# Strassen blocks added to x as woven work, and the second layer's query latent in one pass over k-tiles 8 to 15, then 0 to 7

## The chip, the core and the metric

One NeuronCore of one Trainium2 chip runs the whole program as one launch. The metric is device microseconds (us) of one execution. PE is TensorE, PEld its weight loads, DVE is VectorE, ACT ScalarE, POOL GpSimd, SP SyncE, whose queue issues nearly all loads. PSUM is used as eight banks of 128 x 512 floats.

## What is computed

A trunk of two layers over 256 tokens (x is 256 x 2048, float32), all weights float32. Each layer, cut to what matters here:

```
h    = rmsnorm(x);  proj = h @ w_in        # 2048 -> 4928: c_q (512), c_kv (256), k_rope (64), rq, rk, rv, rg
mix  = concat(rmsnorm(latent attention(c_q, c_kv, k_rope)), retention(rq, rk, rv, rg))
x    = x + mix @ w_o
h    = rmsnorm(x)
x    = x + square(relu(h @ w_up)) @ w_down # 2048 -> 8192 -> 2048
```

After the second layer there is a last rmsnorm. `c_q` is the query latent.

## The kernel before

x stays on the chip, transposed, as 16 tiles `x[0]` to `x[15]` of 128 features x 256 tokens. Every weight passes once through the same line (`stream`, L216): SP loads 512 KB into one of five `raw` buffers, ACT rounds it to a high half (L195), DVE subtracts to get the low half (L196), both into one of six `w` buffers, and PE multiplies. I call that a chunk and its two halves its split. `mac_feat` (L227) is one pair of matmuls: L229 takes the weight's high half against both halves of the activation (512 columns), L230 the low half against one (256 columns). An activation tile `xs[j]` is made from `x[j]` by `norm_tile` (L333: ACT L191, DVE L192). The sum of squares that the norm needs is gathered by `add_square` (L267: ACT L272, DVE L273 into `ssq`); the norm itself is applied later, as row factors (`scale_rows`, L399; its first matmuls are L306).

The MLP runs in four blocks of 2048 hidden features. In each, `w_up` gives 16 tiles `us`; then `w_down` is done in two ways. Output tiles 0 to 7 come from a Strassen step: eight times (k = 0 to 7) 21 matmuls of 512 columns (`seven_products`, L722, matmul L730) into seven banks, from sums and differences of the weights that DVE makes in place in `raw` (L716). Output tiles 8 to 15 are plain, each 16 pairs over two chunks (`next_tile`, L808), placed between the Strassen steps. In the last block of a layer the seven sums are joined on DVE (`join_products`, L740, L747) into four 128 x 512 blocks of tokens, and `add_blocks` (L750) adds those to `x[0]` to `x[7]`: for each tile two transposes on PE (L756) into a bank and one DVE addition (L757), then `done_x` (L674), which makes `xs` and the square for the next layer. In that last block the sums of blocks 0 to 2 are joined and added once more, before the second `w_up` group (L787).

At the end of a layer six plain tiles stand behind steps k = 0 to 5 (`LAST_TILE_AFTER`); after step 7 come tile 14, `add_blocks`, tile 15. In the second layer the latent `cq` then takes two passes (L368 and L369) of two output tiles each over all k-tiles, in chunks of four k-tiles from the back (12 to 15 first). Then follow the 320 columns of c_kv and k_rope (L380 to L385), which I call the kv stage, and rq, rk, rv, rg.

Tasks that need little PE are written as generators and put in `woven`; `stream` calls `weave` (L201) after each chunk's matmuls, and each call runs one generator to its next `yield`.

The order on each engine is not that of the source alone. A list scheduler of the framework orders instructions by its own costs when the program is built, and each engine then runs its queue strictly in that order, waiting on semaphores. So the order is read from the built program.

## Time and profile before

| | |
|---|---|
| median of 3 runs | 2172.16 us (2171.90 to 2172.17) |
| the profiled execution, its own time | 2172.12 us |
| its span | 2170.3 us (1.8 us lie around it) |
| PE, DVE, ACT busy | 98%, 82%, 60% of the span |
| largest stretch with PE waiting | 1059 to 1094 us, the change of layers |

The profile's page gives the averages; a window view gives busy time and the granted PE clock of a stretch; the timeline gives each instruction's start and duration, with the idle time ahead of it and what ended it in brackets. Successive instructions of one engine overlap in the records: the step from start to start is what one costs in a row, and the duration is a little more.

### The profile page before, as it was taken

How to read it: one execution, taken by the hardware profiler on the slowest of the kernel's cores; microseconds unless marked ns; L12 is line 12 of the kernel's file. 1: busy time of each engine (PE TensorE's matmuls, PEld its weight loads, DVE VectorE, ACT ScalarE, POOL GpSimd, SP SyncE). 2: the span in 40 equal slices, each digit the busy share in tenths (PEclk: the TensorE clock that was granted, in tenths of full speed). 3: DMA queues.
4: the chain of work that ended last, by engine and by line, in shares of the span. 5: the costliest groups of instructions: out<-in, count | busy, mean ns of one | idle time of the engine just before them, and what ended most of it. 6: DMA issues, size and time to landing. Idle time of an engine off the chain costs nothing.

```text
span 2170.3 us, 32892 instructions
## 1 busy us (share of the span) xinstructions
PE 2135.7 (98%) x11926; PEld 1861.6 (86%) x11926; DVE 1789.4 (82%) x3183; ACT 1300.3 (60%) x2234; POOL 107.0 (5%) x130
## 2 busy tenths in 40 slices
PE   7999999999999999999899999999999999999997
PEld 6888888888888888888688888888888888888886
DVE  8878976788689779879968888676986887898797
ACT  7455545565676566566645555456665655665665
POOL 4000000001001001100000000000010010010000
PEclk9999999999999999999999999999999999999998
DMA  7555456658757857855465555566587577577663
GB/s 247 171 161 174 147 189 196 184 168 227 235 165 216 241 165 217 247 176 173 148 200 159 165 173 165 183 189 186 169 236 219 167 224 236 165 217 224 181 194 107
DMA packets 364771, 412.69 MB, mean 190 GB/s; under 512 B 14144, under 2 KB 284608, under 8 KB 364608
## 3 DMA queue, kind: packets, MB, share of 16 engines
q1 hardware_dynamic: 349824, 397.08, 59.7%
q0 software_dynamic: 13824, 12.59, 3.9%
q8 instruction: 93, 1.52, 0.3%
q10 hardware_dynamic: 960, 0.92, 0.1%
q14 instruction: 70, 0.57, 0.1%
HBM read 395.85 MB, written 2.10 MB: 183 GB/s over the span
## 4 chain that ended last, share of the span: by engine, by line
PE 88%; DVE 7%; ACT 2%; issue 1%; DMA 1%; SPq 0%; DVEq 0%; ACTq 0%
PE mm L229 43%; PE mm L230 22%; PE mm L730 11%; PE mm L234 3%; DVE w L196 2%; DVE raw L716 2%; PE mm L235 1%; PE at L229 1%; ACT w L195 1%; DMA raw<-w_down 1%; PE at L230 1%; PE at L500 0%; PE at L499 0%; PE mm L383 0%; PE mm L384 0%
## 5 line engine op out<-in xcount | busy, mean ns | idle before, releaser
L195 ACT CAST w<-raw 128x1024 fp32r<-128x1024 f32 (+2 forms) x856 | 847.1, 1007 | 656.8 <-PE mm L230 363.2
L196 DVE TENSOR_TENSOR w<-raw,w 128x1024 fp32r<-128x1024 f32 (+2 forms) x856 | 987.1, 1170 | 291.9 <-ACT w L195 286.1
L229 PE MATMUL mm<-xs,w 128*128 128x512 f32 x2944 | 1034.2, 394 | 8.5 <-ACT w L195 8.3
L230 PE MATMUL mm<-xs,w 128*128 128x256 f32 x2944 | 827.4, 281 | 4.4 <-DVE w L196 4.4
L229 PEld LDWEIGHTS mm<-xs,w 128*128 128x128 f32 x2944 | 553.8, 188 | 127.8 <-ACT w L195 8.6
L230 PEld LDWEIGHTS mm<-xs,w 128*128 128x128 f32 x2944 | 556.0, 189 | 7.5 <-DVE w L196 7.1
L229 PE MATMUL mm<-u,w 128*128 128x512 f32 x1024 | 360.7, 393 | 0.2 <-ACT w L195 0.2
L230 PE MATMUL mm<-u,w 128*128 128x256 f32 x1024 | 288.8, 282 | 6.4 <-DVE w L196 6.4
L229 PEld LDWEIGHTS mm<-u,w 128*128 128x128 f32 x1024 | 193.2, 189 | 43.0 <-ACT w L195 0.7
L230 PEld LDWEIGHTS mm<-u,w 128*128 128x128 f32 x1024 | 194.0, 189 | 10.0 <-DVE w L196 7.3
L730 PE MATMUL mm<-w,f 128*128 128x512 f32 x768 | 191.1, 396 | 2.2 <-ACT w L195 1.2
L716 DVE TENSOR_TENSOR raw<-raw 128x512 f32<-128x512 f32 x256 | 176.8, 691 | 6.6
L229 PE MATMUL mm<-mix,w 128*128 128x512 f32 x512 | 178.0, 391 | 0.0
L730 PEld LDWEIGHTS mm<-w,f 128*128 128x128 f32 x768 | 144.0, 188 | 38.9 <-ACT w L195 2.1
L820 POOL DMA_DIRECT2D x<-t x96 | 83.4, 869 | 1863.0 <-ACT t L819 1561.9
L230 PE MATMUL mm<-mix,w 128*128 128x256 f32 x512 | 143.7, 281 | 0.0
L247 ACT COPY tb<-mm 128x256 f32<-128x256 f32 x232 | 82.5, 371 | 63.0 <-PE mm L230 59.3
L229 PEld LDWEIGHTS mm<-mix,w 128*128 128x128 f32 x512 | 96.1, 188 | 20.8
L730 PE MATMUL mm<-w,u 128*128 128x512 f32 x384 | 110.6, 396 | 0.0
L248 DVE TENSOR_TENSOR t<-mm,tb 128x256 f32<-128x256 f32 x232 | 91.4, 418 | 19.9 <-ACT tb L247 19.4
L230 PEld LDWEIGHTS mm<-mix,w 128*128 128x128 f32 x512 | 96.4, 188 | 0.0
L234 PE MATMUL mm<-w,xs 128*128 128x512 f32 x256 | 92.8, 401 | 0.0
(202 smaller groups left out, 1955.3 us busy)
## 6 DMA issues: line engine op xcount, KB each, us to landing
raw<-w_up SPq DMA_DIRECT2D x256, 512.0 KB, 4.4
raw<-w_down SPq DMA_DIRECT2D x256, 512.0 KB, 5.2
raw<-w_in SPq DMA_DIRECT2D x144, 512.0 KB, 4.5
raw<-w_o SPq DMA_DIRECT2D x64, 512.0 KB, 4.1
x<-t POOLq DMA_DIRECT2D x96, 128.0 KB, 5.7
raw<-w_uq SPq DMA_DIRECT2D x16, 384.0 KB, 4.3
raw<-w_in SPq DMA_DIRECT2D x16, 320.0 KB, 3.2
raw<-w_ukv SPq DMA_DIRECT2D x8, 512.0 KB, 4.3
```

Of the source, the lines that this page charges most:

```text
L195: nc.scalar.copy(dst_h, src)
L196: nc.vector.tensor_tensor(dst_l, src, dst_h.bitcast(F32), op=ALU.subtract)
L229: nc.tensor.matmul(ps, wk[:, 0, n0:n0 + P], act.rearrange("p s t -> p (s t)"), start=first, stop=False)
L230: nc.tensor.matmul(ps[:, 0:T], wk[:, 1, n0:n0 + P], act[:, 0, :], start=False, stop=last)
L234: nc.tensor.matmul(ps, act[:, 0, t0:t0 + P], wk, start=first, stop=False)
L235: nc.tensor.matmul(ps[:, 0:256], act[:, 1, t0:t0 + P], wk[:, 0], start=False, stop=last)
L247: nc.scalar.copy(tb, ps[:, T:2 * T])
L248: nc.vector.tensor_tensor(dst, ps[:, 0:T], tb, op=ALU.add)
L716: nc.vector.tensor_tensor(dst, dst, other, op=ALU.add)
L730: nc.tensor.matmul(ps[i], a[:, p, :], w[:, q, :], start=first and n == 0, stop=last and n == 2)
L820: nc.gpsimd.dma_start(x[j], t, accum_op=ALU.add)
```

## The change

`add_blocks` becomes a generator that yields ahead of every second (or third) tile, so that its transposes and additions are woven between chunks. It is used so in three places: for blocks 0 to 2 inside the second `w_up` group of each layer's last block; at the end of layer 1 inside the latent of layer 2; at the end of layer 2 inside plain tiles 14 and 15 (three tiles a piece). In layer 1 seven plain tiles stand behind steps 0 to 6, and tile 15 follows step 7. The latent of layer 2 is one pass of four output tiles, in chunks of two k-tiles, over k-tiles 8 to 15, then 0 to 7, built at the end of layer 1. The squares of x for layer 2 are no longer made in `done_x`; they are woven into the kv stage, in the order 8 to 15, 0 to 7.

```diff
-TILE_AFTER, LAST_TILE_AFTER = range(8), range(6)
+TILE_AFTER, LAST_TILE_AFTER = range(8), (range(7), range(6))
-    def stream(w, r0, c0, nk, width=256, kc=None, backward=False):
+    def stream(w, r0, c0, nk, width=256, kc=None, first=0):
-        for s in reversed(range(0, nk, kc)) if backward else range(0, nk, kc):
+        for s in [*range(first, nk, kc), *range(0, first, kc)]:
...
+    def first_squares(first):
+        for i, j in enumerate([*range(first, KD), *range(first)]):
+            if i % 4 == 0:
+                yield
+            add_square(acc, x[j], i == 0)
+    latent = None
...
-            if l == 0:
-                woven["a"].append(first_squares())
+            woven["a"].append(first_squares(SN if l else 0))
...
-                for ps in proj_feat(w_in[l], 0, c0, xs, backward=l > 0):
+                for ps in proj_feat(w_in[l], 0, c0, xs) if latent is None else [latent.pop(0) for _ in range(2)]:
...
                 if not last_layer:
                     xs_n[j] = norm_tile(j, (l + 1) * G_LAYER + G_ATTN)
-                    add_square(acc_n, x[j], not squared)
...
-            def add_blocks(blocks, final=True):
+            def add_blocks(blocks, final=True, start=0, step=2):
                 for n in range(2):
                     for f in range(SB // P):
                         j = n * (SB // P) + f
+                        if j == start:
+                            start += step
+                            yield
                         xT = abank()
...
                     if end and c == 4:
-                        add_blocks(join_products(sums, sums), False)
+                        woven["a"].append(add_blocks(join_products(sums, sums), False))
...
-                    if k in (LAST_TILE_AFTER if end else TILE_AFTER):
+                    if k in (LAST_TILE_AFTER[l] if end else TILE_AFTER):
                         next_tile()
...
                 if end:
                     blocks = join_products(pp, sums)
-                    while len(tiles) > 1:
-                        next_tile()
-                    add_blocks(blocks)
+                    if last_layer:
+                        woven["a"].append(add_blocks(blocks, step=3))
                 else:
                     gather_products(pp, sums, b == 0)
                 while tiles:
                     next_tile()
+            if not last_layer:
+                woven["a"].append(add_blocks(blocks))
+                next(woven["a"][0])
+                latent = proj_feat(w_in[l + 1], 0, COL_CQ, xs_n, 4, SN)
+            finish("a")
             acc, xs = acc_n, xs_n
```

The places in the built order that the prediction speaks of follow. The numbers behind the names tell buffers apart (`x6_85` is the pair of tiles 6 and 7, `p4` a joined block, `mm` and `at` banks); `w<-raw,w` of shape 128x8x128 is the low half of a plain tile's chunk, 128x2x512 that of a chunk of the latent with the change.

DVE, before, at the change of layers: the low half of tile 15's second chunk, with the last of what stands ahead of it.

```order
L273 TENSOR_TENSOR ssq_4164<-ssq_4164,sq_10948 128x256
L192 SCALAR_TENSOR_TENSOR xs5_10955<-x4_81,gain_73,xs5_10955 128x256
L273 TENSOR_TENSOR ssq_4164<-ssq_4164,sq_10958 128x256
L757 TENSOR_TENSOR x6_85<-x6_85,at_10961 128x256
L757 TENSOR_TENSOR x6_85<-x6_85,at_10971 128x256
L196 TENSOR_TENSOR w_11005<-raw_11003,w_11005 128x8x128
L192 SCALAR_TENSOR_TENSOR xs6_10965<-x6_85,gain_73,xs6_10965 128x256
```

DVE, with the change, at the same place: from tile 15's first chunk to the latent's second.

```order
L196 TENSOR_TENSOR w_10885<-raw_10883,w_10885 128x8x128
L248 TENSOR_TENSOR t_10825<-mm_10782,tb_10826 128x256
L747 TENSOR_TENSOR p2_5855<-p1_5853,mm_10182 128x512
L817 TENSOR_TENSOR x14_101<-x14_101,t_10825 128x256
L196 TENSOR_TENSOR w_10906<-raw_10904,w_10906 128x8x128
L196 TENSOR_TENSOR w_10939<-raw_10937,w_10939 128x2x512
L192 SCALAR_TENSOR_TENSOR xs14_10830<-x14_101,gain_73,xs14_10830 128x256
L747 TENSOR_TENSOR p6_5863<-p1_5853,mm_10186 128x512
L196 TENSOR_TENSOR w_10974<-raw_10972,w_10974 128x2x512
```

Between the two chunks of tile 15 stood 24 additions, low halves of `xs` and squares; now three additions stand there.

PE, before, at the end of the program, in the middle of tile 15: `keep_warm`'s matmuls (L850), which the scheduler put there.

```order
L229 MATMUL mm<-u_20503,w 128x512
L230 MATMUL mm<-u_20503,w 128x256
L229 MATMUL mm<-u_20696,w 128x512
L850 MATMUL mm<-u_20189,u_20199 128x512 x13
L230 MATMUL mm<-u_20696,w 128x256
L229 MATMUL mm<-u_20706,w 128x512
```

PE, with the change, at the end of tile 15 (L857 is `keep_warm`, L759 the transposes).

```order
L229 MATMUL mm<-u_21043,w 128x512
L230 MATMUL mm<-u_21043,w 128x256
L759 MATMUL at<-cst,p_16662 128x128
L857 MATMUL mm<-u_20189,u_20199 128x512 x8
L306 MATMUL at<-ones,ssq 128x1
L857 MATMUL mm<-u_20189,u_20199 128x512 x6
L306 MATMUL at<-ones,sq 128x1
```

The 13 matmuls left the tile, and the last transpose of `x[7]` now follows it.

DVE, with the change, behind the kv stage of layer 2: the last square, the copies out of the kv stage's banks, and the first instruction of the row factors (L308).

```order
L273 TENSOR_TENSOR ssq_4164<-ssq_4164,sq_11334 128x256
L196 TENSOR_TENSOR w_11621<-raw_11631,w_11621 128x128
L392 COPY kv_nat_11389<-mm_11204 128x256
L395 COPY kv_nat_11389<-mm_11204 128x2x32 x2
L392 COPY kv_nat_11390<-mm_11205 128x256
L395 COPY kv_nat_11390<-mm_11205 128x2x32 x2
L308 TENSOR_SCALAR v6_11449<-at_11451 128x2
```

Fifteen additions of squares moved here from the end of layer 1; before, the copies stood ahead of the 128x128 low halves, and no square was near.

## Rows read from the trace of the kernel before

**Rows 1.** The page, busy time of each engine: us (share), instructions.

```profile
PE 2135.7 (98%) x11926; PEld 1861.6 (86%) x11926; DVE 1789.4 (82%) x3183; ACT 1300.3 (60%) x2234; POOL 107.0 (5%) x130
```

**Rows 2.** Who PE waited for, 1053 to 1113 us: us in total, times, longest.

```profile
PE mm L230 <- DVE w L196: 8.0, 2, 6.4
```

**Rows 3.** Windows: us, busy of PE, PEld, DVE, ACT, POOL; clock, DMA share, GB/s.

```profile
1053.68:1112.77 59.09, 49.17 (x252) 40.71 (x251) 45.90 (x75) 31.98 (x55) 0.00 (x0) 0.91 0.52 152
...
1083.92:1089.21 5.29, 5.29 (x18) 4.61 (x19) 4.81 (x7) 0.67 (x2) 0.00 (x0) 0.50 0.62 171
1112.77:1132.40 19.63, 19.63 (x130) 18.99 (x129) 14.03 (x25) 12.01 (x23) 0.00 (x0) 1.00 0.82 240
...
922.13:932.13 10.00, 9.87 (x63) 8.70 (x62) 9.57 (x29) 8.14 (x19) 0.00 (x0) 1.00 0.28 70
```

**Rows 4.** Timeline of PE, change of layers: start, us, instruction, count, idle before.

```profile
1053.68 0.86 PE L730 MATMUL mm<-wh,u 128*128 128x512 f32 x3
1054.38 0.86 PE L730 MATMUL mm<-w,u 128*128 128x512 f32 x3
...
1067.12 0.39 PE L229 MATMUL mm<-u,w 128*128 128x512 f32 x1
...
1072.32 1.69 PE L756 MATMUL at<-cst,p 128*128 128x128 f32 x14
...
1083.92 0.58 PE L230 MATMUL mm<-u,w 128*128 128x256 f32 x1 [6.42 <-DVE w L196]
...
1112.77 0.31 PE L383 MATMUL mm<-w,xs 128*128 128x320 f32 x1
```

**Rows 5.** Timeline of DVE, change of layers.

```profile
1050.68 2.86 DVE L716 TENSOR_TENSOR raw<-raw 128x512 f32<-128x512 f32 x4
1053.46 2.50 DVE L196 TENSOR_TENSOR w<-raw,w 128x1024 fp32r<-128x1024 f32 x2
1055.88 0.42 DVE L248 TENSOR_TENSOR t<-mm,tb 128x256 f32<-128x256 f32 x1
1056.21 0.68 DVE L196 TENSOR_TENSOR wh<-raw,wh 128x512 fp32r<-128x512 f32 x1
...
1058.28 0.48 DVE L192 SCALAR_TENSOR_TENSOR xs<-x,gain,xs 128x256 fp32r<-128x256 f32 x1
...
1068.49 3.08 DVE L747 TENSOR_TENSOR p<-p,mm 128x512 f32<-128x512 f32 x5
...
1072.63 0.75 DVE L757 TENSOR_TENSOR x<-x,at 128x256 f32<-128x256 f32 x2
...
1082.64 1.22 DVE L196 TENSOR_TENSOR w<-raw,w 128x1024 fp32r<-128x1024 f32 x1
```

**Rows 6.** Timeline of PE, a break of four transposes in the retention of layer 2.

```profile
1188.10 0.60 PE L595 MATMUL at<-cst,on 128*128 128x128 f32 x4
1188.45 0.48 PE L229 MATMUL mm<-xs,w 128*128 128x512 f32 x1
```

**Rows 7.** The page, DMA issues: count, size, median us from issue to landing.

```profile
raw<-w_in SPq DMA_DIRECT2D x144, 512.0 KB, 4.5
```

**Rows 8.** Timeline of PE, blocks 0 to 2 added in layer 1's last block.

```profile
922.13 1.91 PE L756 MATMUL at<-cst,p 128*128 128x128 f32 x16
924.17 0.50 PE L229 MATMUL mm<-xs,w 128*128 128x512 f32 x1
```

**Rows 9.** Timeline of PE, end of the program.

```profile
2144.52 1.91 PE L756 MATMUL at<-cst,p 128*128 128x128 f32 x16
...
2149.30 3.15 PE L850 MATMUL mm<-u,u 128*128 128x512 f32 x13
...
2156.83 0.38 PE L306 MATMUL at<-ones,sq 128*128 128x1 f32 x2 [1.37 <-ACT sq L683]
```

**Rows 10.** Timeline of DVE, end of the program: tile 15's second split.

```profile
2150.72 1.22 DVE L196 TENSOR_TENSOR w<-raw,w 128x1024 fp32r<-128x1024 f32 x1
```

**Rows 11.** Timeline of ACT, end of the program.

```profile
2156.36 0.42 ACT L683 ACTIVATE sq<-x 128x256 f32<-128x256 f32 x1 [0.95 <-DVE x L814]
```

More of the change, by code (lines that the diff above doesn't have):

```diff
@@ L235, in mac_tok, with proj_feat @@
         nc.tensor.matmul(ps[:, 0:256], act[:, 1, t0:t0 + P], wk[:, 0], start=False, stop=last)
-    def proj_feat(w, r0, c0, acts, nt=2, backward=False):
+    def proj_feat(w, r0, c0, acts, nt=2, first=0):
         ps = [bank() for _ in range(nt)]
         nk = len(acts)
-        for i, (k, wk) in enumerate(stream(w, r0, c0, nk, nt * P, backward=backward)):
+        for i, (k, wk) in enumerate(stream(w, r0, c0, nk, nt * P, first=first)):
             for n in range(nt):
@@ L343 @@
         xs[j] = norm_tile(j, G_ATTN)
-    def first_squares():
-        for j in range(KD):
-            if j % 4 == 0:
+    def first_squares(first):
+        for i, j in enumerate([*range(first, KD), *range(first)]):
+            if i % 4 == 0:
                 yield
-            add_square(acc, x[j], j == 0)
+            add_square(acc, x[j], i == 0)
+    latent = None
     for l in range(DEPTH):
```

## The prediction

> **What bounds the kernel now.** I read four views in this order: the page, the waits of PE, windows over the stretches with waits, and the timelines of PE, DVE and ACT there. On the page PE is busy nearly throughout [rows 1], so only two kinds of gain are left: time in which PE waits, and PE work that could go. The waits of PE over the change of layers [rows 2] name one cause above all: the low half of a weight chunk, made by DVE, 8.0 us in two waits. The timeline shows the large one [rows 4]: 6.42 us at 1083.92, in the middle of plain tile 15. What DVE did instead stands in its own timeline [rows 5]: the low half that PE wants is started only at 1082.64, behind the 24 additions, xs and squares that begin at 1072.63. The window behind the wait [rows 3] then shows a second price: the granted clock is 0.50, the lower level of 1.2 GHz, for 5.29 us after the engine stood idle 6.42 us.
>
> **The change of layers, worked out.** What PE has to do between 1053.68 (first product of step 6) and 1112.77 (first matmul of the kv stage) [rows 4]:
> - 42 products of steps 6 and 7. Three take 0.70 us from start to start, so 0.233 each: 9.8 us.
> - 96 pairs (tiles 14 and 15: 32; the latent: 64). From 1067.12 to 1072.32 there are 15: 0.347 each, 33.3 us.
> - 16 transposes. Four in a break take 0.35 us, and the first matmul behind them 0.48 instead of 0.39 us [rows 6]: 0.45 for four, 1.8 us.
> - 0.1 us for each tile's slower first pair (as in [rows 6]), 0.2.
>
> The sum is 45.1 us, and the stretch took 59.09 [rows 3]: 14.0 us are lost. Of these 8.0 are the two waits for DVE [rows 2], 2.2 the lower clock (18 matmuls in 5.29 us where nine pairs take 3.1), and the remaining 3.8 short waits in step 7, where DVE has four additions in raw and four low halves to make in 4.9 us of PE.
>
> With the change the same PE work stands there, with the same loads, only in another order: tile 14 between steps 6 and 7, the transposes in four pieces. Will PE wait again? I add up DVE's queue in its new order, each instruction at its full duration [rows 5], which is an upper bound, since in a row they overlap by about a tenth. It is free of step 6 at 1055.96 (1053.46 + 2.50). Up to tile 15's second low half come seven low halves of 1024 columns (1.25), one of 512 (0.68), four additions in raw (2.86), two joins and two additions to x (0.42 each), one xs (0.48), one joined block (0.62): 15.1 us, so 1071.0. PE wants it after 21 + 21 products, tile 14 and half of tile 15: 1053.68 + 9.8 + 5.55 + 2.8 + 0.2 = 1072.0. In time by 1 us at the worst, by 2.4 if the overlap is counted. The latent's first transposes, at 1077.6, want the last joined block: 6.7 us more of DVE, 1077.7 at the worst, 1075.8 with the overlap. The fourth chunk, at 1084.4, wants xs[15]: 5.8 us more, 1083.5 at the worst. SP's queue holds as many loads as before; tile 14's two now go ahead of step 7's, and the latent's eight are 512 KB each as they were. Each needs the buffer that DVE gave back five loads earlier: the latent's second chunk that of step 7's first load, free by 1066 at the worst, and it lands 4.5 us later [rows 7], 1070.5, where DVE comes to it at 1073 or later. Nothing is late by more than some tenths, so I take **14.0 us gained** (kv stage from 1098.8). Bounds: 14.0 above, and 8.8 below, should 3 us of waits come back with their 2.2 us of lower clock.
>
> **The squares, moved.** Fifteen additions of squares and two more latent tiles (join, xs, square) land on DVE in the kv stage. DVE is busy 14.03 of the 19.63 us up to the first row-factor matmul at 1132.40 [rows 3]. 15 times 0.34 (0.42 less the overlap) and 2 times 1.05 are 7.2, so 21.2 us, less 1.2 for the copies that now stand behind the squares: 20.0 in 19.6. ACT, at 12.0, gets the same squares and tiles at about the same price, 19.2, and has a little room. So the row factors' matmul waits some tenths, and what follows it on DVE starts later by the copies. I put **0.5 us lost** here; bounds 0 and 4 (none of the excess is hidden, and the factors' broadcast is late too).
>
> **The blocks inside w_up.** Sixteen transposes in one burst take 2.04 us to the next matmul, and that one is 0.1 slower [rows 8]; four breaks of four are 1.8 [rows 6]. This occurs once in each layer: **0.5 us gained** in all, bounds 0.6 gained and 0.6 lost (a wait of 0.1 in each of the new breaks). DVE's additions there are the same in number, and PE did not wait before.
>
> **The end.** Tile 15 held 13 matmuls of keep_warm, 3.0 us [rows 9]. They hid a wait: its second low half is started at 2150.72 [rows 10], ready at 2151.9, while PE wanted it at 2149.3. In the new order it stands behind eight instructions of at most 0.42 instead of sixteen: begun at 2144.9, behind the first transposes, they and the low half take 4.6 us at the worst, 3.8 with the overlap: ready at 2148.7 to 2149.5. PE, with 15 transposes and eight pairs ahead, is there at 2149.1, so it waits 0.4 at most. So tile 15 ends at 2144.52 + 16 x 0.347 + 1.9 for transposes = 2152.0 instead of 2154.8. Not all of it reaches the end: the last transpose of x[7] now follows the tile, and ACT squares x[7] ahead of the copy with which tile 15's join begins. From 2152.0: transpose 0.3, then addition, square, copy, join, addition at about 0.4 each, with 0.3 between them: the last square starts at 2154.6 to 2154.8, before at 2156.36 [rows 11]. **1.6 us gained**; bounds 0 (the low half is as late as before, and PE waits for it) and 2.8 (the whole tile's).
>
> **The sum.** The profiled execution's own time is 2172.12 us, the median of the runs shown 2172.16, so one stands for the other. 2172.1 - 14.0 + 0.5 - 0.5 - 1.6 = **2156.5 us**. A measurement of this kernel can tell about 0.2%, 4.3 us, from no change.
>
> **The rivals.**
> - *DVE is still late at the change of layers.* The stretch has 45.9 us of DVE work [rows 3]; less about eleven squares' additions of 0.42 some 41 remain in 45.1, so there is little room, and a buffer or a load that comes late moves the whole queue. For it: my upper bounds leave 1 us or less. Against: they are upper bounds, and six steps before it lose a square each. Waits of 3 us and 2.2 us of clock: 2161.7.
> - *The squares hold up the row factors.* ACT and DVE wait for each other by turns on two buffers of squares, so the excess of 0.4 us may be 4: 2160.0.
> - *Slower: breaks of transposes lower the clock.* The place is every break that the change makes, four in each w_up group and four in the latent. After the idle time the lower level cost 0.24 us a pair (2.2 over nine). If each of the 12 breaks costs the eight pairs up to the next one that, it is 96 x 0.24 = 23.0 us: 2179.5. It decides from 16 / 0.24 = 66 pairs on. Against: in the window of 10 us from 922.13, which begins with the burst of 16, the clock is 1.00 [rows 3].
> - *It does not do what it says:* the wait only moves (to the kv stage's first chunks, say), and the time stays at 2172.
>
> On the third of these the Trainium skill speaks (TensorE: Matmul & The Clock Gate, Part 4: PE-mode transpose): the full clock does not engage for transposes, since they do not count as busy in the same way. By that rule the breaks would be idle time and the third rival would hold, 2179.5 instead of 2156.5. The one row that bears on it disagrees: 16 in a row, longer than any new break, left the clock at 1.00.
>
> **How the numbers follow.** My forecast, 2154.3 to 2158.5, has 0.65 (its width: 0.6 either way for the w_up groups, 1 for the end, 1 for the squares). Squares late by more: 0.12, 2158.5 to 2160.5. DVE still late: 0.12, 2160 to 2165, half of it below 2162. Clock: 0.03. No change: 0.03. Better than I count: 0.05. The range 2154.3 to 2162.0 holds 0.65 + 0.12 + 0.06 = 0.83. Faster by over 0.2% are all but the clock, the unchanged case: 0.94; within 0.2%: 0.03; slower: 0.03.
>
> **What would show it.** Right: PE's waits from 1053 to 1100 us below 1 us in all, the kv stage's first matmul near 1098.8, the clock at 1.00 throughout there, keep_warm's matmuls behind tile 15, the row factors' first matmul 5.5 to 6.5 us behind the last of the kv stage. Wrong: a wait for a low half in tile 15 or the latent (first rival); idle PE ahead of L306 or of the factors' broadcast (second); a clock below 1.00 with no idle time ahead of it (third); pairs in the latent slower than 0.35 us.

## The result, and the profile after

| | before | after |
|---|---|---|
| median | 2172.16 us (2171.90 to 2172.41, 4 runs) | 2154.28 us (2153.87 to 2154.59, 4 runs) |
| the profiled execution, its own time | 2172.12 us | 2153.87 us |
| its span | 2170.3 us | 2152.1 us |

The ratio is 0.9916, 95% interval 0.9904 to 0.9928: faster by 17.9 us, where 15.6 were forecast, so the time lies 0.02 us under the range that was given (2154.3 to 2162.0), and the forecast was off by 2.2 us. The direction, the place and the largest term were right; the term of the end was too small by 1 us, and the other small terms were off to the same side.

The page of the changed kernel, busy time of each engine, answers [rows 1]:

```profile
PE 2130.2 (99%) x11926; PEld 1860.1 (86%) x11926; DVE 1786.9 (83%) x3183; ACT 1301.6 (60%) x2234; POOL 108.0 (5%) x130
```

The instructions are the same in number. PE's busy time fell by 5.5 us, its idle time by the rest of the 18.2 us between the spans (which are printed to 0.1 us, so a stretch that ends with the program is good to 0.05 us). Who PE waited for over the whole program (us in total, times, longest):

```profile
PE mm L229 <- ACT w L195: 7.6, 1, 7.6
PE mm L230 <- DVE w L196: 3.2, 2, 2.5
PE at L322 <- DVE rs_y L295: 1.6, 1, 1.6
```

The first two lie in the first 24 us of the program, the third at its end. At the change of layers, where 8.0 us stood [rows 2], nothing is left. The windows from step 6 to the kv stage, and from there to the row factors' first matmul, answer [rows 3] (columns as there):

```profile
1053.10:1097.96 44.86, 44.86 (x252) 39.02 (x251) 39.34 (x60) 25.89 (x39) 0.00 (x0) 1.00 0.67 200
1097.96:1117.72 19.76, 19.76 (x130) 18.90 (x129) 19.03 (x39) 18.20 (x41) 0.00 (x0) 1.00 0.77 235
```

PE is busy in all of the 44.86 us, at a clock of 1.00. Its timeline there answers [rows 4]:

```profile
1063.53 0.86 PE L730 MATMUL mm<-wh,u 128*128 128x512 f32 x3
...
1068.42 0.39 PE L229 MATMUL mm<-u,w 128*128 128x512 f32 x1
...
1076.75 0.60 PE L759 MATMUL at<-cst,p 128*128 128x128 f32 x4
...
1079.97 0.60 PE L759 MATMUL at<-cst,p 128*128 128x128 f32 x4
```

1063.53 is step 7, 1068.42 tile 15, and two of the four breaks of transposes in the latent (L759; L756 before) follow. From one break to the next are 3.22 us: eight pairs of 0.347 and 0.44 for the break. DVE's timeline, with [rows 5]:

```profile
1062.04 3.64 DVE L196 TENSOR_TENSOR w<-raw,w 128x1024 fp32r<-128x1024 f32 x3
...
1066.91 2.35 DVE L196 TENSOR_TENSOR w<-raw,w 128x1024 fp32r<-128x1024 f32 x2
...
1071.32 3.07 DVE L747 TENSOR_TENSOR p<-p,mm 128x512 f32<-128x512 f32 x5
...
1077.24 0.74 DVE L760 TENSOR_TENSOR x<-x,at 128x256 f32<-128x256 f32 x2
...
1096.19 0.82 DVE L196 TENSOR_TENSOR w<-raw,w 128x640 fp32r<-128x640 f32 x1 [1.95 <-ACT w L195]
```

The row at 1066.91 is tile 15's second low half and the latent's first. The former is done by some 1068.1 and PE wants it at 1071.2, eight pairs into the tile; before the change it was begun at 1082.64. By 1096 DVE is ahead of PE and waits for ACT. Before the change not all of the 10.0 us ahead of that low half was work; 1.32 us went by in waiting for a copy of ACT:

```profile
1074.70 0.42 DVE L248 TENSOR_TENSOR t<-mm,tb 128x256 f32<-128x256 f32 x1 [1.32 <-ACT tb L247]
```

The stretches, each from the starts of the same instructions in the two timelines of PE:

| stretch | before | after | difference | forecast |
|---|---|---|---|---|
| start to the second w_up group of layer 1's last block | 899.92 | 899.72 | -0.20 | |
| that group (blocks 0 to 2), to step 0 | 90.97 | 90.58 | -0.39 | -0.25 |
| step 6 to the kv stage | 59.09 | 44.86 | -14.23 | -14.0 |
| kv stage to the row factors' first matmul, and the factors | 20.45 | 20.65 | +0.20 | +0.5 |
| the w_up group of layer 2, to step 0 | 90.96 | 90.65 | -0.31 | -0.25 |
| steps 6 and 7 of layer 2 | 10.56 | 9.88 | -0.68 | |
| tile 14 of layer 2 to the end | 31.45 | 28.85 | -2.60 | -1.6 |

The other stretches agree within 0.02 us; the sum is 18.2 us, the difference of the spans.

The end on PE, with [rows 9]; tile 14 begins at 2123.25, where before it began at 2138.85:

```profile
2133.28 0.49 PE L759 MATMUL at<-cst,p 128*128 128x128 f32 x3
2136.16 0.27 PE L759 MATMUL at<-cst,p 128*128 128x128 f32 x1
2136.19 2.10 PE L857 MATMUL mm<-u,u 128*128 128x512 f32 x8
...
2138.26 1.63 PE L857 MATMUL mm<-u,u 128*128 128x512 f32 x6
2139.73 0.28 PE L306 MATMUL at<-ones,sq 128*128 128x1 f32 x2
...
2142.03 0.68 PE L322 MATMUL at<-cst,rs_y 128*128 128x128 f32 x4 [1.57 <-DVE rs_y L295]
```

and on ACT, with [rows 11]:

```profile
2138.62 0.42 ACT L683 ACTIVATE sq<-x 128x256 f32<-128x256 f32 x1 [0.61 <-DVE x L817]
2139.07 0.51 ACT L686 ACTIVATE x<-x,gain 128x256 f32<-128x256 f32 x1
2139.60 1.28 ACT L289 ACT_TABLE_LOAD   x1
2140.90 0.20 ACT L289 ACTIVATE rs_r<-nv 128x2 f32<-128x2 f32 x1
```

The last square starts 15.37 us behind tile 14's start, before 17.51. From there on another 0.5 us is gained: the four L322, which spread the last norm's factors, took 1.19 us before, at a clock of 0.50, and now 0.68:

```profile
2159.77 1.19 PE L322 MATMUL at<-cst,rs_y 128*128 128x128 f32 x4 [2.11 <-DVE rs_y L295]
```

### The profile page after: what moved, and what is told of

The parts are those of the page before. It is cut to its first block, busy times and chain, and to the rows that moved or that the text cites. A ratio compares the mean times of both kernels' runs of the same rounds, so it can differ in the third digit from the quotient of the medians.

```text
span 2152.1 us, 32894 instructions
## 1 busy us (share of the span) xinstructions
PE 2130.2 (99%) x11926; PEld 1860.1 (86%) x11926; DVE 1786.9 (83%) x3183; ACT 1301.6 (60%) x2234; POOL 108.0 (5%) x130
## 4 chain that ended last, share of the span: by engine, by line
PE 98%; ACT 1%; DVE 1%; DMA 0%; issue 0%; SPq 0%; DVEq 0%
PE mm L229 47%; PE mm L230 25%; PE mm L730 15%; PE mm L234 3%; PE mm L235 1%; PE at L229 1%; PE at L230 1%; PE at L501 0%; PE at L500 0%; PE mm L385 0%; PE mm L384 0%; PE mm L386 0%; PE at L234 0%; PE at L533 0%; PE at L562 0%; PE at L759 0%
## 5 line engine op out<-in xcount | busy, mean ns | idle before, releaser
L229 PE MATMUL mm<-xs,w 128*128 128x512 f32 x2944 | 1035.7, 394 | 7.7 <-ACT w L195 7.6
L230 PE MATMUL mm<-xs,w 128*128 128x256 f32 x2944 | 827.7, 281 | 3.2 <-DVE w L196 3.2
L229 PEld LDWEIGHTS mm<-xs,w 128*128 128x128 f32 x2944 | 554.2, 188 | 126.3 <-ACT w L195 8.0
L230 PEld LDWEIGHTS mm<-xs,w 128*128 128x128 f32 x2944 | 556.2, 189 | 5.1 <-DVE w L196 4.8
L229 PE MATMUL mm<-u,w 128*128 128x512 f32 x1024 | 358.6, 391 | 0.0
L230 PE MATMUL mm<-u,w 128*128 128x256 f32 x1024 | 287.5, 281 | 0.0
L229 PEld LDWEIGHTS mm<-u,w 128*128 128x128 f32 x1024 | 192.2, 188 | 42.1
L230 PEld LDWEIGHTS mm<-u,w 128*128 128x128 f32 x1024 | 192.9, 188 | 3.1 <-DVE w L196 0.3
L229 PE MATMUL mm<-mix,w 128*128 128x512 f32 x512 | 178.0, 391 | 0.0
L230 PE MATMUL mm<-mix,w 128*128 128x256 f32 x512 | 143.7, 281 | 0.0
L229 PEld LDWEIGHTS mm<-mix,w 128*128 128x128 f32 x512 | 96.1, 188 | 20.8
L230 PEld LDWEIGHTS mm<-mix,w 128*128 128x128 f32 x512 | 96.4, 188 | 0.0
```

What stands on the lines that cost most here:

```text
L229: nc.tensor.matmul(ps, wk[:, 0, n0:n0 + P], act.rearrange("p s t -> p (s t)"), start=first, stop=False)
L230: nc.tensor.matmul(ps[:, 0:T], wk[:, 1, n0:n0 + P], act[:, 0, :], start=False, stop=last)
```

## Experiments

The theory: at the change of layers a low half stood too far back in DVE's queue, twice over (in step 7, and behind the burst in tile 15), and the lower clock followed. The rivals: that DVE's work there was simply too much (then moving the squares is the gain), that the tile between the steps is, that the latent's new pass is, or that pieces of transposes are needed or harmful. Each run's profile gives the stretch from step 6 to the kv stage, which repeats to hundredths in the kernels that have no wait there; whole times of one kernel lie 0.5 us to over 3 us apart, in part because the program's start differs: the same matmul starts at 36.0 us in one profile and at 38.0 in another.

**Parts undone in the changed kernel.** The squares back in `done_x`:

```diff
-            woven["a"].append(first_squares(SN if l else 0))
+            if l == 0:
+                woven["a"].append(first_squares(0))
...
                     xs_n[j] = norm_tile(j, (l + 1) * G_LAYER + G_ATTN)
+                    add_square(acc_n, x[j], not squared)
```

> The changed kernel, but the squares of x for layer 2 are made in done_x again and not in the kv stage. Theory (what counts is where DVE's queue puts the low half that PE wants next): in the built order tile 15's second low half now stands behind five joined blocks, one low half of xs and one square, 3.5 to 4 us of DVE that stood behind it in the changed kernel, and there it was ready only 0.1 us before PE wanted it. So PE waits 2.5 to 4 us at L230 in tile 15, the clock may fall behind that wait, and the time is 2156.5 to 2160. The kv stage gives back 0.2 us. Rival A (the squares are too much work for DVE in this stretch in any order, and moving them was most of the gain): several waits in the latent, 2161 or more. Rival B (the squares are hidden wherever they stand): no wait, 2154 to 2155.

Measured: 2155.25 us, ratio to before 0.9922 (0.9907 to 0.9936); step 6 to the kv stage 45.80 us, +0.94. The theory named the place and was wrong on the size. The low half did come late: DVE began it at 1073.02, PE's first chunk of tile 15 was done at 1071.9. But PE had other work, as its timeline shows:

```profile
1071.65 0.39 PE L229 MATMUL mm<-u,w 128*128 128x512 f32 x1
1071.88 1.10 PE L229 MATMUL mm<-xs,w 128*128 128x512 f32 x4
1072.82 0.99 PE L761 MATMUL at<-cst,p 128*128 128x128 f32 x6
1074.29 0.38 PE L230 MATMUL mm<-u,w 128*128 128x256 f32 x1 [0.48 <-DVE w L196]
```

Between tile 15's first L229 of the second chunk and its L230 the scheduler put four L229 of the latent and six transposes, which need no low half. Of the lateness of 2.4 us PE waited 0.48; what the rest of the 0.94 is no wait shows. The expectation had this low half ready 0.1 us ahead of PE in the changed kernel; its trace has 3.1 us. Here weaving gave PE something to do, besides moving DVE's additions.

Tile 14 behind step 7 in layer 1:

```diff
-TILE_AFTER, LAST_TILE_AFTER = range(8), (range(7), range(6))
+TILE_AFTER, LAST_TILE_AFTER = range(8), (range(6), range(6))
```

> The changed kernel, but layer 1 has tile 14 behind step 7 again, with tile 15. Theory: step 7 directly behind step 6 asks DVE for four additions in raw and four low halves in 4.9 us of PE work, which DVE cannot give, so the short waits of step 7 come back, 3 to 4 us in all; the built order keeps tile 15's second low half clear of the 24 instructions that it stood behind before the change, so the wait of 6.4 us does not come back. Time 2157 to 2158.5. Rival A (the place of the tile is most of the gain): the wait in tile 15 and the lower clock come back, 2163 or more. Rival B (DVE has the time anyway): no wait, 2154 to 2155.

Measured: 2154.43 us, 0.9919 (0.9904 to 0.9934); 45.53 us, +0.67, and no wait that the profile names. The theory fell here: the waits of step 7 stay away without the tile. Both parts undone together:

```diff
-            woven["a"].append(first_squares(SN if l else 0))
+            if l == 0:
+                woven["a"].append(first_squares(0))
...
-TILE_AFTER, LAST_TILE_AFTER = range(8), (range(7), range(6))
+TILE_AFTER, LAST_TILE_AFTER = range(8), (range(6), range(6))
```

> The changed kernel with two parts undone together: the squares are made in done_x, and layer 1 has tile 14 behind step 7. Each alone cost 0.9 and 0.7 us. Theory (the two parts are two cures of one thing, DVE's lateness at step 7, and stand in for each other): without both the short waits of step 7 come back, 3 to 4 us, while tile 15 and the latent stay free of waits: 48 to 49.5 us from step 6 to the kv stage, 2157 to 2158.5. Rival A (the two add up): 46.5 us, 2155.8. Rival B (with the squares in the latent too, DVE no longer keeps up): waits in the latent as well, 51 us or more, 2160 or more.

Measured: 2157.26 us, 0.9926 (0.9909 to 0.9942); 48.18 us, +3.32 where the two alone make 1.61. PE's waits from step 6 to the kv stage are step 7's again, those of the kernel before:

```profile
PE mm L732 <- ACT w L195: 1.2, 2, 0.7
PE mm L732 <- DVE w L196: 0.5, 1, 0.5
PE mm L229 <- ACT w L195: 0.2, 1, 0.2
```

So the two parts are cures of one thing and stand in for each other, as the theory had it. Neither rival holds: they do not add up, and with the squares in the stretch DVE still keeps up with the latent. How the squares cure step 7 shows in DVE's first addition in raw for it, here and in the run just above (tile 14 behind step 7), from which this one differs by the squares alone:

```profile
1058.71 1.41 DVE L718 TENSOR_TENSOR raw<-raw 128x512 f32<-128x512 f32 x2
1056.51 0.68 DVE L716 TENSOR_TENSOR raw<-raw 128x512 f32<-128x512 f32 x1
```

Step 6 begins on PE at 1053.41 here and at 1053.12 there, so with the squares moved DVE begins 3.4 us behind it instead of 5.3.

The blocks in a burst between tiles 14 and 15 again, with the squares moved and the latent in one pass:

```diff
-TILE_AFTER, LAST_TILE_AFTER = range(8), (range(7), range(6))
+TILE_AFTER, LAST_TILE_AFTER = range(8), (range(6), range(6))
...
+                    else:
+                        while len(tiles) > 1:
+                            next_tile()
+                        for _ in add_blocks(blocks):
+                            pass
...
-                woven["a"].append(add_blocks(blocks))
-                next(woven["a"][0])
```

> The changed kernel, but at the end of layer 1 the order is that of before: tile 14 behind step 7, then the blocks in one burst, then tile 15; the latent is one pass and the squares are in the kv stage as in the change. Theory (the burst ahead of tile 15's second low half is the cause that only weaving cures): 17 instructions of some 0.42 us stand ahead of that low half, PE waits 4 to 5 us at L230 in tile 15, and the clock behind it falls to its lower level for some 2 us more: 51 to 53.5 us from step 6 to the kv stage, 2160.5 to 2163. Rival (the latent's order and pass or the squares carried the gain): 44.9 to 47 us, 2154.3 to 2156.5.

Measured: 2160.74 us, 0.9945 (0.9929 to 0.9962); 51.67 us, as the theory had it. PE in tile 15:

```profile
1079.33 0.50 PE L230 MATMUL mm<-u,w 128*128 128x256 f32 x1 [3.21 <-DVE w L196]
1079.63 0.63 PE L229 MATMUL mm<-u,w 128*128 128x512 f32 x1
1080.05 0.41 PE L230 MATMUL mm<-u,w 128*128 128x256 f32 x1
1080.27 0.63 PE L229 MATMUL mm<-u,w 128*128 128x512 f32 x1
```

and the window behind the wait:

```profile
1079.33:1084.60 5.27, 5.27 (x23) 4.62 (x24) 4.20 (x6) 0.85 (x2) 0.00 (x0) 0.68 0.72 199
```

The clock of 0.68 is the mean of five slow pairs and the faster ones behind them. The wait is 3.21 us, shorter than the 4 to 5 expected, and behind it a pair takes 0.64 us instead of 0.35, for five pairs. Against the run with tile 14 behind step 7 alone (45.53 us), the burst costs 6.1 us: neither the moved squares nor the new latent cures it.

The transposes in the same place as in the change, but behind one chunk:

```diff
             if not last_layer:
-                woven["a"].append(add_blocks(blocks))
+                woven["a"].append(add_blocks(blocks, step=8))
```

> The changed kernel, but the eight blocks' transposes at the change of layers all come behind the latent's first chunk instead of two tiles behind each of four chunks (in the built order eight in a burst, the others one pair of matmuls apart). Theory (the place counts, not the pieces): the low halves of the latent's first four chunks stand ahead of the burst on DVE, the fifth is wanted some 3 us after the burst is done, so no wait, the clock stays at 1.00, and PE's own time differs by tenths: 44.7 to 45.4 us from step 6 to the kv stage, 2154 to 2155. Rival A (many transposes lower the clock or the burst's additions hold up a low half, so pieces are needed): 2 us or more lost, 2156.3 or more, with a wait at L230 in the latent or a clock below 1.00 there.

Measured: 2154.02 us, 0.9917 (0.9902 to 0.9931); 44.93 us, no wait, clock 1.00. The place counts, not the pieces, as far as this run goes: on PE eight of the sixteen transposes stand in a row, on DVE all the additions and `xs` of the blocks, with no low half between them. The latent in two passes:

```diff
-                latent = proj_feat(w_in[l + 1], 0, COL_CQ, xs_n, 4, SN)
+                latent = [p for c0 in range(COL_CQ, COL_CKV, 256) for p in proj_feat(w_in[l + 1], 0, c0, xs_n, 2, SN)]
...
-                woven["a"].append(add_blocks(blocks))
+                woven["a"].append(add_blocks(blocks, step=4))
```

> The changed kernel, but the latent of layer 2 takes two passes of two output tiles, both over k-tiles 8 to 15, then 0 to 7, and the blocks come in two breaks of eight transposes behind its first two chunks. Theory: x[0] to x[7] are now wanted after 16 instead of 32 pairs behind tile 15, 5.6 us sooner; by DVE's queue xs[0] is ready about a microsecond before PE wants it and xs[7] within half a microsecond of it, so 0 to 1.5 us are lost: 44.8 to 46.4 us from step 6 to the kv stage, 2154 to 2156. Rival (one pass is what gives DVE the time): 2.5 us or more lost, with waits at L229 for xs in the first pass, 2156.8 or more.

Measured: 2153.96 us, 0.9911 (0.9897 to 0.9926); 44.87 us, no wait. The one pass, one of the two things that the change is named for, is worth nothing here as long as the order begins with the k-tiles 8 to 15 and the blocks are woven; and the stretch from the kv stage to the factors is 20.44 us with two passes, where one pass has 20.65.

**Parts alone, in the kernel before.** The squares:

```diff
-                    add_square(acc_n, x[j], not squared)
...
+            if l:
+                woven["a"].append(first_squares())
             nkv = COL_RQ - COL_CKV
```

> The kernel before, with one part of the change: the squares of x for layer 2 are woven into the kv stage. Theory: the loss at the change of layers had two causes. DVE, loaded to the full in steps 0 to 5, came late to step 7 (3.8 us of short waits), and tile 15's second low half stood behind the burst of the blocks (6.4 us, a second wait of 1.6 us and 2.2 us of lower clock). Without squares DVE is about a microsecond earlier at step 6, so the first goes; of the 24 instructions between tile 15's chunks 17 are left, so of the 6.4 us some 4.4 stay, and the clock still falls. From step 6 to the kv stage 53 to 55 us instead of 59.1 (45 with the whole change), time 2165.5 to 2168. Rival A (the squares' work on DVE is what was too much): 45 to 47 us, 2158 to 2160. Rival B (squares are hidden): 58 us or more, 2171 to 2173.

Measured: 2166.73 us, 0.9975 (0.9966 to 0.9985); 54.02 us, -5.07. PE's waits there:

```profile
PE mm L230 <- DVE w L196: 5.8, 2, 4.7
PE mm L731 <- ACT w L195: 0.3, 1, 0.3
```

Step 7 waits 0.3 us instead of 1.7, tile 15 waits 4.66 instead of 6.42, and the time is in the range expected. The tile:

```diff
-TILE_AFTER, LAST_TILE_AFTER = range(8), range(6)
+TILE_AFTER, LAST_TILE_AFTER = range(8), (range(7), range(6))
```

> The kernel before, with one part of the change: in layer 1 tile 14 follows step 6, and step 7, the burst of the blocks and tile 15 come behind it. Theory: the short waits of step 7 go, but the burst now starts as soon after step 7 as DVE has joined the blocks, with all 24 instructions and the joins ahead of tile 15's second low half; PE gets there sooner and waits as much longer, 8 to 11 us at L230. From step 6 to the kv stage 57 to 61 us, time 2170 to 2174. Rival A (a tile between the steps gives DVE its time, and that was the gain): 47 us or less, 2160 or less. Rival B (3.8 us gone, the rest as it was): 55.3 us, 2168.4.

Measured: 2170.19 us, 0.9991 (0.9982 to 1.0); 58.10 us, -0.99. PE's waits:

```profile
PE mm L230 <- DVE w L196: 7.0, 2, 6.1
PE at L756 <- DVE p L747: 2.4, 2, 2.2
```

No wait of step 7 is left, yet what went there came back: PE reaches the burst sooner and waits 2.4 us for the joined blocks, and 6.10 for tile 15's low half; at L230 it waits 7.0 us in all, where 8 to 11 were expected. By itself the tile nearly only moves the wait.

**The w_up groups.**

```diff
-                        woven["a"].append(add_blocks(join_products(sums, sums), False))
+                        for _ in add_blocks(join_products(sums, sums), False):
+                            pass
```

> The changed kernel, but blocks 0 to 2 are added at once inside w_up, in one burst of sixteen transposes, as before the change. Theory (DVE, which is busy without a break through the steps behind w_up, carries a delay from there to the end of the layer): PE itself loses 0.3 to 0.4 us in each w_up group, and DVE comes 0.6 to 0.7 us later to steps 6 and 7, so that the wait of 0.5 us in step 7 of layer 2 comes back and PE waits some 0.6 us at the change of layers too: 1.5 to 2 us in all, 2155.8 to 2156.3. Rival (only PE's own time of the transposes differs): 0.5 to 0.8 us in all, steps 6 and 7 of layer 2 at 9.9 us as in the changed kernel, 2154.8 to 2155.1.

Measured: 2155.07 us, 0.9922 (0.9907 to 0.9936). The groups take 90.96 and 90.95 us again, +0.38 and +0.30; the change of layers 44.87, as without it. The time is the rival's: the half of the theory that had DVE late there as well fell. Steps 6 and 7 of layer 2 took 10.23 us; but in the ten other kernels of this study that keep the woven groups the same stretch reads from 9.79 to 10.69, though the source differs in nothing there but one square root, and in the five with the burst from 10.23 to 10.65. The 0.68 us of the table is not settled.

**The end.** As before the change:

```diff
-                        woven["a"].append(add_blocks(blocks, step=3))
+                        while len(tiles) > 1:
+                            next_tile()
+                        for _ in add_blocks(blocks):
+                            pass
```

> The changed kernel, but at the end of layer 2 the blocks are added in one burst between tiles 14 and 15, as before the change. Theory: from the start of tile 14 to the end of the program 31.4 us as before the change instead of 28.9, so 2156.7 to 2157.0; keep_warm's matmuls stand in tile 15 again, PE is idle ahead of the last L306 and of L322, and the four L322 take some 1.2 us instead of 0.7. Rival (part of the 2.6 us came from DVE or the loads being earlier at the end through the other edits): 1 to 2 us come back, 2155.3 to 2156.3.

Measured: 2156.40 us, 0.9929 (0.9911 to 0.9945); from tile 14 to the end 31.48 us, L322 1.20, as the theory had it; the whole time lies 0.3 us under what it expected. And alone, in the kernel before:

```diff
+                        if j % step == 0:
+                            yield
...
-                    while len(tiles) > 1:
-                        next_tile()
-                    add_blocks(blocks)
+                    if last_layer:
+                        woven["a"].append(add_blocks(blocks, step=3))
+                    else:
+                        while len(tiles) > 1:
+                            next_tile()
+                        for _ in add_blocks(blocks):
+                            pass
```

> The kernel before, with one part of the change: at the end of layer 2 the blocks are woven into tiles 14 and 15, three a piece. Theory: the end's gain stands by itself: 28.9 us from the start of tile 14 to the end of the program instead of 31.45, PE's time up to there as before, 2169.3 to 2169.9. Rival (the end needs the earlier DVE that the other edits give): 29.8 us or more, 2170.5 or more.

Measured: 2170.41 us, 0.999 (0.9981 to 0.9999); from tile 14 to the end 29.35 us, -2.10. The last square comes at the same 15.35 us as in the change, so that part stands by itself. But L322 took 1.20 us although keep_warm's matmuls stand behind tile 15 in the same order: the other 0.5 us is not certain in every execution. (In this profile the change of layers, untouched, took 61.10 us instead of 59.09, its second wait 2.60 instead of 1.6; that is why this execution's own time, 2171.04 us, shows less.)

```diff
-    keep_warm(8)
...
-    keep_warm(6)
```

> The changed kernel without the fourteen matmuls of keep_warm (L857), whose results nothing uses. Theory (a part of the gain at the end that was not foreseen is that these matmuls now stand behind tile 15 and keep the clock at its upper level for the last matmuls): with PE idle for some 2.5 us behind tile 15 the four L322 take about 1.2 us instead of 0.7, as before the change, and the last multiplications start 0.5 us later: from the start of tile 14 to the end 29.2 to 29.5 us instead of 28.85. Rival A (they count for nothing): 28.8 us. Rival B (six of them stand in the way of the last L306 and delay it by 0.6 us): 28.2 to 28.5 us.

Left out are fourteen matmuls that no output uses. Measured: 2155.11 us, 0.9917 (0.9902 to 0.9931); from tile 14 to the end 29.25 us, +0.40, and the four L322:

```profile
2143.02 1.22 PE L322 MATMUL at<-cst,rs_y 128*128 128x128 f32 x4 [2.02 <-DVE rs_y L295]
```

With the matmuls behind the tile they took 0.68 to 0.75 us in nine profiles of ten; without, 1.22. Pieces of four:

```diff
-                        woven["a"].append(add_blocks(blocks, step=3))
+                        woven["a"].append(add_blocks(blocks, step=4))
```

> The changed kernel with four instead of three blocks a piece at the end of layer 2, so that no transpose stands behind tile 15 and x[7] is squared before tile 15's join. Theory: the last square, which starts 15.4 us behind the start of tile 14, starts 0.6 to 0.9 us sooner, and so does all that follows: from the start of tile 14 to the end 28.0 to 28.3 us instead of 28.85, 2153.4 to 2153.7. Rival (four additions at once hold up tile 15's second low half, as the burst did): PE waits 0.5 to 1 us at L230 in tile 15 and nothing is gained, 28.8 us or more.

Measured: 2157.18 us, 0.9927 (0.9912 to 0.9942); 31.67 us, +2.82: the whole gain of the end is lost. The rival had it, by a larger amount and without a wait that shows. PE in tile 15:

```profile
2132.78 1.03 PE L759 MATMUL at<-cst,p 128*128 128x128 f32 x8
2133.57 0.48 PE L229 MATMUL mm<-u,w 128*128 128x512 f32 x1
2133.89 3.37 PE L857 MATMUL mm<-u,u 128*128 128x512 f32 x14
2137.10 0.28 PE L230 MATMUL mm<-u,w 128*128 128x256 f32 x1
```

and DVE:

```profile
2135.54 1.22 DVE L196 TENSOR_TENSOR w<-raw,w 128x1024 fp32r<-128x1024 f32 x1
```

The second low half is begun 12.1 us behind tile 14's start, as before the change (11.87 [rows 10]); in the change it is 8.81. The scheduler filled the hole with keep_warm's matmuls, and no wait is shown: the same picture as before the change. One more block a piece undoes the end's gain, by the mechanism of its term.

Last, what still bounds the end:

```diff
-                    nc.scalar.sqrt(root, ones)
+                    nc.scalar.sqrt(root, rows["rs2b"][:, 0:1])
...
-    keep_warm(6)
+    keep_warm(3)
```

> The changed kernel with two more edits: the square root that is taken early, for its table alone, reads a value of layer 2's MLP, so that in the built order it stands there and not at the start of the program, and the table load behind the last square is gone; and keep_warm's second group has three matmuls instead of six. Theory (behind the last square the chain runs over ACT's scaling of x[15], 0.5 us, and the table load, 1.28 us, beside the last L306, 0.7 us behind six matmuls): without the load and with three matmuls fewer L306 begins right behind the last square, and the square root 0.8 to 0.9 us sooner: from the start of tile 14 to the end 27.9 to 28.2 us instead of 28.85, and 2153.2 to 2153.6 if nothing else differs. Rival A (the chain waits for something else, or the clock falls because keep_warm is shorter): 28.7 us or more. Rival B (the load in the MLP holds up PE there): a wait for ACT in layer 2's MLP, 2154.5 or more.

Measured: from tile 14 to the end 28.07 us, as the theory said, and no wait in the MLP. ACT at the end:

```profile
2139.78 0.42 ACT L683 ACTIVATE sq<-x 128x256 f32<-128x256 f32 x1 [0.61 <-DVE x L817]
2140.23 0.51 ACT L686 ACTIVATE x<-x,gain 128x256 f32<-128x256 f32 x1
2141.30 0.20 ACT L289 ACTIVATE rs_r<-nv 128x2 f32<-128x2 f32 x1 [0.57 <-DVE nv L308]
```

The table load is gone and the square root now waits for L308. The two edits are not parted by a run. In the changed kernel L308 ended at 2140.65:

```profile
2140.49 0.16 DVE L308 TENSOR_SCALAR nv<-at 128x2 f32<-128x2 f32 x1 [1.90 <-PE at L306]
```

The square root began at 2140.90, so by these rows the load alone held it up by 0.25 us at most (an estimate); the rest of the 0.78 us needs the three matmuls fewer as well. The whole time, 2154.86 us, 0.992 (0.9907 to 0.9934), does not show the 0.8 us, which is under the spread of the runs (2154.28 to 2155.30); the start of this execution was 0.9 us slower. No version was measurably faster than the change.

## Why the prediction missed its range, and what of it held

**The step that failed** is the term of the end. It was put at 1.6 us and measured 2.60. The working stopped at the last square and put what follows at nothing. In the trace the last square comes 2.14 us sooner, and behind it the four L322 take 0.68 us instead of 1.19, since keep_warm's matmuls now stand behind tile 15; in the run that leaves these matmuls out they take 1.22. With 2.6 for 1.6 the forecast's own sum would be 2155.5, inside its range; the time lies under it by 0.02 us, far less than runs of one kernel differ, so it is the 1 us that counts here and not the edge.

**The change of layers** is the step that carried the result, and it held: 14.23 us for 14.0. The price list gave 45.1 us, and 44.86 were measured; the 0.2 us are its slower first pairs, which do not show. DVE's queue was to have tile 15's second low half ready 1 us ahead of PE at the worst; in the trace it is 3.1 us ahead. Two things were wrong in the reading. The 3.8 us of "short waits in step 7" are a remainder: the profile names 1.9 us of waits there (1.2, 0.5 and 0.2). That these few waits cost more than they last is seen with the squares and the tile both undone: the same 1.9 us of waits, and a stretch that is 3.3 us longer. And the shares of the parts were not told. The stretch from step 6 to the kv stage in eight forms, each from a run (where the blocks are woven, and in the fourth row, the latent is that of the change; elsewhere that of before):

| squares moved | tile 14 between the steps | blocks woven | us |
|---|---|---|---|
| no | no | no | 59.09 |
| no | yes | no | 58.10 |
| yes | no | no | 54.02 |
| yes | no | no, latent of the change | 51.67 |
| no | no | yes | 48.18 |
| no | yes | yes | 45.80 |
| yes | no | yes | 45.53 |
| yes | yes | yes | 44.86 |

The weaving together with the new latent gives 10.9 of the 14.2 us by itself; no run has the weaving with the latent of before. With the squares moved the latent alone is worth 2.4 us and the weaving behind it 6.1. The squares are worth 5.1 without the weaving and 0.9 as the last step, the tile 1.0 and 0.7. The prediction thought of the squares as a cost (0.5 us in the kv stage) with a small help to DVE; they are also a cure of step 7, which DVE reaches earlier without one addition in each of the six steps ahead.

**The squares in the kv stage**: forecast 0.5 us lost, measured 0.20, and not for the squares alone. With the squares moved and the latent in two passes the stretch from the kv stage to the factors takes 20.44 us (two runs), as it does with one pass and the squares in `done_x`; only both together give 20.65. DVE is busy 19.03 us of 19.76 where 20.0 were summed up, ACT 18.20 where 19.2 were.

**The blocks inside w_up** gave 0.70 for 0.5 us: a burst with the slowed pair behind it was taken at 2.1 and is that, four breaks at 1.8 and are 1.75; the sum, 0.7, had been rounded down, and the measured 0.70 lies above the bound of 0.6 that was given.

**The end**, in its parts. The mechanism of the tile (its second low half late, keep_warm's matmuls in the hole) was right, and the run with pieces of four shows it from the other side. Two sizes were off. PE was through with tile 15's pairs 12.91 us behind tile 14's start, where 13.15 were summed up, and from there to the last square went 2.46 us, where 2.6 to 2.8 were; together these make the last square 2.14 us sooner instead of 1.6. The other 0.5 us is L322, at which the working did not look. It is not certain in every execution: in one of ten profiles with the matmuls behind the tile the clock was 0.50 and L322 took 1.20 us, and why is open. The bound above (2.8, the whole tile's) held the sum of both, but by luck: it was worked out without the second.

**Not in the sum** were 0.2 us at the start and 0.68 in steps 6 and 7 of layer 2, which vary as much between kernels that are alike there; their cause is open. With the end's 1.0, the change's 0.2, the squares' 0.3 and the groups' 0.2 they make the difference of the two profiled executions.

**The rivals.** DVE is not late: there is no wait. The rival of late row factors is out as well. The slower rival, breaks of transposes that lower the clock, is out too: the clock is 1.00 over a stretch with four such breaks, and also in the run with eight transposes in a row, and a break costs 0.44 us. The Trainium skill (TensorE: Matmul & The Clock Gate, Part 4: PE-mode transpose), by which the full clock does not engage for transposes, is not borne out here: these transposes stand among matmuls, and no row shows a lower clock behind them. Whether they run in the mode that the page speaks of, no row tells.

## What to carry to other kernels

When an engine that is behind serves one that waits, read what stands ahead of the awaited instruction in its queue: a burst of cheap additions in the wrong place cost 6.1 us here with the squares and the latent as in the change, and the same additions, in one piece on DVE too, behind the latent's first chunk nothing. Cures of one wait stand in for each other, so a part's worth is known only from both sides, alone and as the last step. A filler that the scheduler may place can hide a wait: look at where filler stands in the trace before believing that an engine was busy with work. And a chain at the end of a program is to be priced to its last instruction: here the half us that was left out lay behind the step at which the working stopped.

## What the runs showed of the hardware

- After idle times of 3.21, 4.66 and 6.42 us PE came back at the lower clock, and a pair took 0.64 us instead of 0.35 for the next five or more pairs; after 1.12 and 0.94 us (in the two runs with the squares or the tile alone) the pairs stayed at 0.35. After about 2.5 us, early in the program, both occur: the clock was 0.50 from 22.47 to 25.40 us after 2.47 us of idle time in the run with tile 14 behind step 7, and 1.00 from 22.34 to 25.00 us after 2.50 us in the run with the burst inside w_up. So the idle time ahead does not by itself tell the clock.
- A table load on ACT costs its 1.28 us and no more in this trace: it starts 0.02 us behind the scaling ahead of it, and the square root 0.02 us behind its end. The Trainium skill (ScalarE: Activation LUTs, What ACT_TABLE_LOAD costs) adds a drain of about 1.38 us to each; no row here shows one, and the measurement decides.
- A square root of a constant, meant to fetch the table early, had been moved to the start of the program by the scheduler, and two other loads undid it. With an input that is ready only in layer 2's MLP the load stays there, at 1455 us; with three of keep_warm's matmuls fewer besides, the end is 0.8 us shorter by the trace.
